# Issuing the gates' and the spilled activations' loads of a PEER layer from ScalarE's queue instead of SyncE's

## The chip, the cores and the metric

The kernel runs on one core of one Trainium2 chip. The metric is the device time of one execution in microseconds (us). A core has five engines that run their own instruction streams in order: TensorE (PE, with its weight loads shown apart as PEld), VectorE (DVE), ScalarE (ACT), GpSimd (POOL) and SyncE (SP). Each stream may also hold instructions that issue a DMA; such an instruction stands in its engine's order like any other, and waits there until the buffer that it fills is free. The profile shows them as SPq, ACTq or POOLq.

## The reference

Two transformer blocks over 512 tokens of 1024 features in float32. The first is differential attention with a hierarchical mixture of experts; the second has a forgetting attention, an RWKV mixer and, at its end, the layer that this case is about: a PEER layer with 16384 single-neuron experts. For each token and head a top-k over product keys picks experts with gates. With the experts numbered in 128 blocks of 128, the layer's output for 384 of the tokens is computed densely:

```
for each block b of 128 experts:
    act[b] = gelu(uT[b]^T x)          # 128 experts x 384 tokens
    W[b]   = act[b] * G[b]            # G: the gates, zero where a token didn't pick the expert
    y     += W[b]^T v[b]              # 384 tokens x 1024
out = layernorm(x * 2^0.25 + y)
```

The last 128 tokens are computed sparsely instead: GpSimd gathers the rows of u and v that each token picked, and VectorE makes the dot products with u and then adds the weighted rows of v.

## The kernel before

Float32 products are made of three matmuls of split operands (`mm3`, L49 to L51: hi x hi, lo x hi, hi x lo). `split` makes the two parts of an operand: the high one on ScalarE (L66), the low one, a subtraction, on VectorE (L67). `load_split` loads a raw tile by `nc.sync.dma_start` (L78) and splits it.

`peer` (L1812) works in two stages. While the gates are being prepared, `spill` computes the activations of the first `NB` = 60 blocks and stores them in DRAM (`hd`); the gates go to DRAM too (`gd`). The last phase is the loop `for z in range(128 + LA)` over all 128 blocks, in the order `order`, which alternates four spilled blocks with four others that are still to be computed (now and then eight of one kind). For each z:

- Every fourth block a tile `G` with the gates of four blocks is loaded (L1917, 768 KB, 2 buffers).
- The block's `act` (3 buffers) is either loaded from `hd` (L1920, 192 KB) or computed by `u_block`: a load of u (512 KB, 3 buffers), its split into `u_hi`, `u_lo`, 24 matmuls of 128x384 into `psu`, and a gelu on ScalarE (L1840).
- VectorE multiplies `act` by the gates in place (L1924); the product is split into `W_hi` (ScalarE) and `W_lo` (VectorE).
- With a lookahead of `LA` = 2, the v of block z - 2 is loaded (512 KB, 3 buffers), split into `v_hi` and `v_lo`, and 18 matmuls of 128x512 add W^T v to the six accumulators `py`.

In between, the steps of the sparse tile are spread over the loop: GpSimd's gathers (L1790), in the first half VectorE's dot products `row<-row,x` (L1797), in the second its sums `x<-row,rg,x` (L1806).

The code is written in the order of the loop; a scheduler puts each engine's instructions in their final order, with the buffers' numbers as its limits. Each engine then runs its list strictly in that order. All loads of the last phase, u, v, G and act, are issued by SyncE.

We call the stretch of eight blocks, four computed and four spilled, a turn. There are 15 turns, some 51 us each; the four computed blocks of a turn are u1 to u4, the four spilled ones s1 to s4. P is the time at which TensorE starts its first `py` matmul after the `psu` matmuls of u4. From P on TensorE has the `py` matmuls of five blocks in a row: u2, u3, u4, s1, s2.

Of the kernel before, what the change touches and what calls it, by code (L numbers as in the profile page):

```python
# [27 lines left out]
class Kern:  # L28
# [1783 lines left out]
    def peer(self, x):  # L1812

        nc, I, tc = self.nc, self.I, self.tc
        NB, ND = 60, NT - 1
        TD = ND * 128
        with ExitStack() as ph:
            dp = ph.enter_context(tc.tile_pool(name="prd", bufs=1, space=DRAM))
            gd = self.t(dp, [2 * ND, 128, 128, 64], F32, "gd")
            hd = self.t(dp, [NB, 128, TD], F32, "hd")  # L1820
# [7 lines left out]
            for kc in range(KC):  # L1828
                p = self.psx()
# [4 lines left out]
            def u_block(b, dst, eng=None):  # L1834

                u = self.load_split(up, I["uT"][b], [128, KC, 128], "u", 3, 3, eng)
                p = self.t(psu, [128, TD], F32, "psu")
                for kc in range(KC):
                    self.mm3(p, [z[:, kc, :] for z in u], [z[:, kc, 0:TD] for z in xT], kc == 0, kc == KC - 1)
                nc.scalar.activation(dst, p, AF.Gelu)  # L1840
# [13 lines left out]
            def run(n):  # L1854
                for step in steps[:n]:
                    step()
                del steps[:n]
# [47 lines left out]
            def blocks(tiles):  # L1905
                for i, W, v in last:
                    for t in tiles:
                        for h in range(2):
                            self.mm3(py[t][h], [y[:, t * 128:(t + 1) * 128] for y in W],
                                     [y[:, h * 512:(h + 1) * 512] for y in v], i == 0, i == 127)  # L1910

            for z in range(128 + LA):
                if z < 128:
                    b = order[z]
                    if b % 4 == 0:
                        G = self.t(wp, [128, 2 * ND, 4, 64], F32, "G", 2)
                        nc.sync.dma_start(G, gd[:, :, b:b + 4, :].rearrange("h p i t -> p h i t"))  # L1917
                    a = self.t(wp, [128, TD], F32, "act", 3)
                    if b < NB:
                        nc.sync.dma_start(a, hd[b])  # L1920
                    else:
                        u_block(b, a)
                    a3 = a.rearrange("p (h t) -> p h t", t=64)
                    nc.vector.tensor_tensor(a3, a3, G[:, :, b % 4, :], OP.mult)  # L1924
                    Ws[b] = self.pair(wp, [128, TD], "W", LA + 3)
                    self.split(Ws[b], a)
                if z >= LA:
                    c = order[z - LA]
                    v = self.load_split(wp, I["v"][c * 128:(c + 1) * 128, :], [128, D], "v", 3, 3)
                    last.append((z - LA, Ws.pop(c), v))  # L1930
                    if z < 128 - 3 + LA:
                        blocks(range(ND))
                        last = []
                    run(len(steps) - max(0, rest - -(-(z - LA + 1) * rest // 122)))
                    if not steps and not ended:
                        ended = True
                        self.layer_norm(wp, x, g, b_, ND, eps)
                        nc.sync.dma_start(self.out[ND * 128:, :], x[:, ND, :])
# [124 lines left out]
```

## Time and profile before

| | |
|---|---|
| median of 3 runs | 2515.73 us (2508.3 to 2515.76) |
| profiled execution, its own time | 2515.3 us |
| its span in the trace | 2513.6 us |
| mean granted clock of TensorE | 0.984 |
| last phase (the loop over 128 blocks) | about 1645 to 2500 us of the span |

The profile is that of one execution, counted from its span's start. An engine's wait is written behind the instruction that followed it, as [us <-what released it]; a table of waits gives for each pair of waiter and releaser the total in us, the number of times and the longest one. In a timeline a row begins with the start and the duration in us; "x2" means two equal instructions back to back, with the time of both.

### The profile page before, as it was taken

How to read it: one execution, taken by the hardware profiler on the slowest of the kernel's cores; microseconds unless marked ns; L12 is line 12 of the kernel's file. 1: busy time of each engine (PE TensorE's matmuls, PEld its weight loads, DVE VectorE, ACT ScalarE, POOL GpSimd, SP SyncE). 2: the span in 40 equal slices, each digit the busy share in tenths (PEclk: the TensorE clock that was granted, in tenths of full speed). 3: DMA queues.
4: the chain of work that ended last, by engine and by line, in shares of the span. 5: the costliest groups of instructions: out<-in, count | busy, mean ns of one | idle time of the engine just before them, and what ended most of it. 6: DMA issues, size and time to landing. Idle time of an engine off the chain costs nothing.

```text
span 2513.6 us, 36164 instructions
## 1 busy us (share of the span) xinstructions
PE 2395.8 (95%) x13502; PEld 1970.5 (78%) x13502; DVE 1924.1 (77%) x3698; ACT 1119.8 (45%) x1651; POOL 553.7 (22%) x458
## 2 busy tenths in 40 slices
PE   8999989999889999999999999989999899999997
PEld 5766666666567777777799989988888789888886
DVE  4577669988867558647699999768787778888786
ACT  3466547777535543224344445533333333333333
POOL 2010112222421100000000000035444444444440
PEclk9999999999999999999999999999999999999999
DMA  7343269999731222225234347899999899999992
GB/s 263 116 166 125 81 228 330 365 366 367 273 105 59 66 72 74 68 60 174 106 115 129 118 151 280 318 360 351 343 336 327 304 331 322 331 338 365 318 334 77
DMA packets 224248, 566.31 MB, mean 225 GB/s; under 512 B 27755, under 2 KB 75924, under 8 KB 223174
## 3 DMA queue, kind: packets, MB, share of 16 engines
q1 hardware_dynamic: 173218, 387.53, 43.7%
q0 software_dynamic: 46048, 166.73, 18.8%
q10 hardware_dynamic: 4804, 9.72, 1.0%
q8 instruction: 107, 1.75, 0.3%
q14 instruction: 71, 0.58, 0.1%
HBM read 511.99 MB, written 51.92 MB: 224 GB/s over the span
## 4 chain that ended last, share of the span: by engine, by line
PE 19%; issue 14%; DVE 12%; POOL 7%; DMA 4%; ACT 1%; POOLq 0%; DVEq 0%; ACTq 0%
POOL row L1790 7%; PE psu L49 3%; PE psu L51 3%; PE psu L50 3%; PE py L50 2%; PE py L51 2%; PE psx L1775 2%; PE py L49 2%; DVE u_lo L67 1%; DMA row<-in_v,ix 1%; DMA act<-hd 1%; DVE x L1806 1%; PE psb L49 1%; PE psb L50 1%; DVE eq L1743 1%
## 5 line engine op out<-in xcount | busy, mean ns | idle before, releaser
L49 PE MATMUL psu<-x4T_hi,u_hi 128*128 128x384 f32 x1024 | 347.1, 339 | 5.6 <-ACT act L1840 4.5
L51 PE MATMUL psu<-x4T_hi,u_lo 128*128 128x384 f32 x1024 | 344.5, 337 | 2.7 <-DVE u_lo L67 2.7
L50 PE MATMUL psu<-x4T_lo,u_hi 128*128 128x384 f32 x1024 | 344.3, 336 | 0.0
L50 PE MATMUL py<-v_lo,W_hi 128*128 128x512 f32 x768 | 303.2, 395 | 17.5 <-DVE v_lo L67 17.5
L49 PE MATMUL py<-v_hi,W_hi 128*128 128x512 f32 x768 | 302.2, 393 | 6.4 <-ACT W_hi L66 5.8
L51 PE MATMUL py<-v_hi,W_lo 128*128 128x512 f32 x768 | 302.3, 394 | 2.2 <-DVE W_lo L67 2.2
L66 ACT ACTIVATE W_hi<-act 128x384 fp32r<-128x384 f32 x128 | 66.4, 525 | 409.1 <-DVE act L1924 408.9
L67 DVE TENSOR_TENSOR ew_lo<-ew_raw,ew_hi 128x2048 fp32r<-128x2048 f32 x93 | 216.8, 2331 | 28.4 <-ACT ew_hi L66 28.3
L1790 POOL DMA_INDIRECT row<-in_v,ix x128 | 181.7, 1420 | 223.4 <-DVE x L1806 189.0
L1790 POOL DMA_INDIRECT row<-in_u,ix x128 | 181.9, 1421 | 222.5 <-DVE dots L1797 204.4
L66 ACT ACTIVATE w_hi<-w_raw 128x1024 fp32r<-128x1024 f32 (+1 forms) x103 | 101.9, 992 | 226.8 <-PE psb L50 147.9
L49 PEld LDWEIGHTS psu<-x4T_hi,u_hi 128*128 128x128 f32 x1024 | 193.3, 189 | 10.1 <-ACT act L1840 4.9
L66 ACT ACTIVATE u_hi<-u_raw 128x1024 fp32r<-128x1024 f32 x128 | 135.0, 1058 | 141.5 <-PE psu L50 124.8
L50 PEld LDWEIGHTS psu<-x4T_lo,u_hi 128*128 128x128 f32 x1024 | 193.4, 189 | 3.7
L51 PEld LDWEIGHTS psu<-x4T_hi,u_lo 128*128 128x128 f32 x1024 | 193.2, 189 | 3.4 <-DVE u_lo L67 3.2
L66 ACT ACTIVATE ew_hi<-ew_raw 128x2048 fp32r<-128x2048 f32 x93 | 178.1, 1916 | 39.8 <-PE psa L51 38.5
L1797 DVE CUSTOM_DVE_ANT_0 row<-row,x 128x1024 f32<-128x1024 f32 x128 | 153.2, 1219 | 45.0 <-DMA row<-in_u,ix 43.5
L50 PEld LDWEIGHTS py<-v_lo,W_hi 128*128 128x128 f32 x768 | 146.0, 190 | 50.4 <-DVE v_lo L67 22.7
L67 DVE TENSOR_TENSOR v_lo<-v_raw,v_hi 128x1024 fp32r<-128x1024 f32 x128 | 156.3, 1221 | 33.3 <-ACT v_hi L66 33.3
L1806 DVE SCALAR_TENSOR_TENSOR x<-row,rg,x 128x1024 f32<-128x1024 f32 x128 | 164.1, 1282 | 18.3 <-DMA row<-in_v,ix 15.2
L49 PEld LDWEIGHTS py<-v_hi,W_hi 128*128 128x128 f32 x768 | 145.7, 190 | 35.6 <-ACT W_hi L66 6.6
L51 PEld LDWEIGHTS py<-v_hi,W_lo 128*128 128x128 f32 x768 | 145.8, 190 | 33.6 <-DVE W_lo L67 3.4
(670 smaller groups left out, 5417.7 us busy)
## 6 DMA issues: line engine op xcount, KB each, us to landing
u_raw<-in_uT SPq DMA_DIRECT2D x128, 512.0 KB
v_raw<-in_v SPq DMA_DIRECT2D x128, 512.0 KB
ew_raw<-in_wgate SPq DMA_DIRECT2D x32, 1024.0 KB
ew_raw<-in_wup SPq DMA_DIRECT2D x32, 1024.0 KB
ew_raw<-in_wdown SPq DMA_DIRECT2D x32, 1024.0 KB
gd<-Gs SPq DMA_DIRECT2D x6, 4096.0 KB
G<-gd SPq DMA_DIRECT2D x32, 768.0 KB
w_raw<-in_w2b SPq DMA_DIRECT2D x39, 512.0 KB
```

The costliest lines, as they stand in the source:

```text
L49: mm(out, L[0], R[0], start=start, stop=False)
L50: mm(out, L[0], R[1], start=False, stop=False)
L51: mm(out, L[1], R[0], start=False, stop=stop)
L66: nc.scalar.activation(hl[0], src, AF.Copy)
L67: (eng or nc.vector).tensor_tensor(hl[1], src, hl[0].bitcast(F32), OP.subtract)
L1743: nc.vector.tensor_tensor(e4, e4, tf[:, s, :, :, None].to_broadcast([128, NT, 16, 16]), OP.mult)
L1775: nc.tensor.matmul(p[:, u, :], A[j], B[i][j], start=i == 0, stop=i == 1)
L1790: keep(nc.gpsimd.indirect_dma_start(r, None, I[name], bass.IndirectOffsetOnAxis(ap=ix[:, h, j:j + 1], axis=0)))
L1797: keep(nc.vector.tensor_tensor_reduce(r, r, x[:, t, :], 1.0, 0.0, OP.mult, OP.add, dots[:, h, j:j + 1]))
L1806: keep(nc.vector.scalar_tensor_tensor(x[:, t, :], r, g[:, h, j:j + 1], x[:, t, :], OP.mult, OP.add))
```

## The change

In the loop of the last phase the loads of G and of the spilled `act` are issued by ScalarE (`nc.scalar.dma_start`) instead of SyncE. These are 32 loads of G and 60 of `act`. The loads of u and v stay on SyncE. No buffer and no arithmetic is changed.

```
--- before.py
+++ after.py
@@ -1914,10 +1914,10 @@
                     b = order[z]
                     if b % 4 == 0:
                         G = self.t(wp, [128, 2 * ND, 4, 64], F32, "G", 2)
-                        nc.sync.dma_start(G, gd[:, :, b:b + 4, :].rearrange("h p i t -> p h i t"))
+                        nc.scalar.dma_start(G, gd[:, :, b:b + 4, :].rearrange("h p i t -> p h i t"))
                     a = self.t(wp, [128, TD], F32, "act", 3)
                     if b < NB:
-                        nc.sync.dma_start(a, hd[b])
+                        nc.scalar.dma_start(a, hd[b])
                     else:
                         u_block(b, a)
                     a3 = a.rearrange("p (h t) -> p h t", t=64)
```

The scheduler's order moves with it. TensorE's and GpSimd's lists have the same instructions as before. In the pieces below, a turn of the second half, act_20277 is the activation of u4, and act_20347, act_20384, act_20421 and act_20458 are those of s1 to s4; v_20430 is the v of s1, v_20467 that of s2 (the numbers differ by one or two between the parts of a tile).

ScalarE's list, from the gelu of u4 on:

```order
 L1840 ACTIVATE act_20277<-psu_20284 128x384
+L1920 DMA act_20347<-hd_11323 128x384
+L1920 DMA act_20384<-hd_11323 128x384
 L66 ACTIVATE W_hi_20311<-act_20277 128x384
-L66 ACTIVATE v_hi_20430<-v_raw_20428 128x1024
+L1917 DMA G_20495<-gd_11322 128x6x256
 L66 ACTIVATE W_hi_20350<-act_20347 128x384
 L66 ACTIVATE W_hi_20387<-act_20384 128x384
+L1920 DMA act_20421<-hd_11323 128x384
+L66 ACTIVATE v_hi_20430<-v_raw_20428 128x1024
+L1920 DMA act_20458<-hd_11323 128x384
+L66 ACTIVATE v_hi_20467<-v_raw_20465 128x1024
```

The loads of s1 and s2 now stand behind the gelu of u4, the load of s3 behind W_hi of s1 and of s2, and the v_hi of s1 and s2 behind the load of s3.

VectorE's list in the same turn, from the multiply of s1 on:

```order
 L1924 TENSOR_TENSOR act_20347<-act_20347,G_20345 128x384
 L1924 TENSOR_TENSOR act_20384<-act_20384,G_20345 128x384
-L67 TENSOR_TENSOR v_lo_20431<-v_raw_20428,v_hi_20430 128x1024
 L67 TENSOR_TENSOR W_lo_20351<-act_20347,W_hi_20350 128x384
 L67 TENSOR_TENSOR W_lo_20388<-act_20384,W_hi_20387 128x384
+L67 TENSOR_TENSOR v_lo_20431<-v_raw_20428,v_hi_20430 128x1024
 L1924 TENSOR_TENSOR act_20421<-act_20421,G_20345 128x384
 L1806 SCALAR_TENSOR_TENSOR x_2268_11033<-row_20452,rg_11399,x_2268_11033 128x1024
 L67 TENSOR_TENSOR W_lo_20425<-act_20421,W_hi_20424 128x384
 L1806 SCALAR_TENSOR_TENSOR x_2268_11033<-row_20455,rg_11399,x_2268_11033 128x1024
+L1924 TENSOR_TENSOR act_20458<-act_20458,G_20345 128x384
 L67 TENSOR_TENSOR v_lo_20468<-v_raw_20465,v_hi_20467 128x1024
```

The v_lo of s2 (v_lo_20468) stands behind the multiply of s3, as before, and now behind the multiply of s4 too.

SyncE's list in the same turn:

```order
 L78 DMA u_raw_20925<-in_uT 128x1024
 L78 DMA v_raw_20535<-in_v 128x1024
-L1920 DMA act_20347<-hd_11323 128x384
-L1920 DMA act_20384<-hd_11323 128x384
 L78 DMA u_raw_20993<-in_uT 128x1024
-L1920 DMA act_20421<-hd_11323 128x384
-L1917 DMA G_20495<-gd_11322 128x6x256
 L78 DMA v_raw_20603<-in_v 128x1024
-L1920 DMA act_20458<-hd_11323 128x384
 L78 DMA v_raw_20674<-in_v 128x1024
-L1917 DMA G_20772<-gd_11322 128x6x256
```

The loads of act and G leave the list, and those of u and v close up.

## Rows read from the trace of the kernel before

**Rows 1.** Windows, the last phase in two halves: columns PE, PEld, DVE, ACT, POOL, PEclk, DMA share, GB/s.
```profile
1650.00:2050.00 400.00, 375.54 (x1789) 329.07 (x1788) 309.80 (x460) 133.27 (x183) 177.40 (x124) 0.98 0.93 336
2050.00:2450.00 400.00, 394.53 (x1902) 347.61 (x1902) 328.21 (x352) 139.91 (x193) 178.94 (x126) 0.99 0.93 333
```

**Rows 2.** Waits of PE from 1640 us on: total, times, longest.
```profile
PE py L50 <- DVE v_lo L67: 17.5, 13, 3.4
PE py L49 <- ACT W_hi L66: 5.8, 1, 5.8
PE psu L49 <- ACT act L1840: 4.5, 1, 4.5
...
PE py L51 <- DVE W_lo L67: 2.2, 1, 2.2
```

**Rows 3.** Timeline of PE, one turn: its P, and v_lo's first use for s2.
```profile
2132.86 0.39 PE L49 MATMUL py<-v_hi,W_hi 128*128 128x512 f32 x1
...
2149.41 0.39 PE L50 MATMUL py<-v_lo,W_hi 128*128 128x512 f32 x1
```

**Rows 4.** Timeline of DVE, the same turn, from the multiply of s3.
```profile
2142.53 0.56 DVE L1924 TENSOR_TENSOR act<-act,G 128x384 f32<-128x384 f32 x1 [2.13 <-DMA act<-hd]
...
2145.87 1.22 DVE L67 TENSOR_TENSOR v_lo<-v_raw,v_hi 128x1024 fp32r<-128x1024 f32 x1
```

**Rows 5.** Tile act: what its engines were idle for (us, times).
```profile
  DMA act<-hd: 50.4, 26
```

**Rows 6.** Timeline of SP, the same turn.
```profile
2131.62 1.06 SPq L1920 DMA_DIRECT2D act<-hd  x2
...
2136.85 0.32 SPq L1920 DMA_DIRECT2D act<-hd  x1
2137.22 0.44 SPq L1917 DMA_DIRECT2D G<-gd  x1
```

**Rows 7.** Waits of SP, 1672 to 2460 us: the largest.
```profile
SPq L78 <- DVE v_lo L67: 376.5, 117, 8.9
```

**Rows 8.** Tile yd, an earlier phase: a DMA that ACT issues, ns min/median/max.
```profile
L952 ACTq DMA_DIRECT2D yd<-yexp x14: 310/310/327, 401.0 to 653.6; - x14
```

**Rows 9.** Timeline of ACT, the same turn: gelu and W_hi of u4.
```profile
2133.85 0.47 ACT L1840 ACTIVATE act<-psu 128x384 f32<-128x384 f32 x1
2135.71 0.53 ACT L66 ACTIVATE W_hi<-act 128x384 fp32r<-128x384 f32 x1 [1.39 <-DVE act L1924]
```

**Rows 10.** Timelines of SP and DVE in the last turn: s1 and s2.
```profile
2389.97 0.90 SPq L1920 DMA_DIRECT2D act<-hd  x2
...
2395.18 1.03 DVE L1924 TENSOR_TENSOR act<-act,G 128x384 f32<-128x384 f32 x2 [0.34 <-DMA act<-hd]
```

**Rows 11.** Timelines of SP and DVE: act issued well behind G.
```profile
1942.31 0.37 SPq L1917 DMA_DIRECT2D G<-gd  x1
1948.95 0.32 SPq L1920 DMA_DIRECT2D act<-hd  x1
...
1954.20 0.56 DVE L1924 TENSOR_TENSOR act<-act,G 128x384 f32<-128x384 f32 x1 [1.13 <-DMA act<-hd]
```

**Rows 12.** Timelines of SP and DVE: act issued 1.6 us behind G (2339.40).
```profile
2341.00 0.32 SPq L1920 DMA_DIRECT2D act<-hd  x1
...
2349.64 0.56 DVE L1924 TENSOR_TENSOR act<-act,G 128x384 f32<-128x384 f32 x1 [5.65 <-DMA act<-hd]
```

**Rows 13.** Timeline of DVE, a turn of the first half: s3's multiply to v_lo.
```profile
1844.82 0.56 DVE L1924 TENSOR_TENSOR act<-act,G 128x384 f32<-128x384 f32 x1 [2.75 <-DMA act<-hd]
...
1849.67 1.22 DVE L67 TENSOR_TENSOR v_lo<-v_raw,v_hi 128x1024 fp32r<-128x1024 f32 x1
```

**Rows 14.** Windows about PE's waits at 1899, 2251 and 2354 us; columns as above.
```profile
1886.00:1906.00 20.00, 17.06 (x69) 13.58 (x68) 14.08 (x24) 6.14 (x9) 6.97 (x6) 0.91 0.82 268
...
2246.00:2256.00 10.00, 8.18 (x30) 6.25 (x29) 8.77 (x10) 3.90 (x5) 4.23 (x4) 0.83 0.86 284
2348.00:2358.00 10.00, 6.94 (x23) 5.08 (x23) 8.37 (x10) 3.89 (x5) 5.04 (x3) 0.83 0.70 235
```

More of the change, by code (lines that the diff above doesn't have):

```diff
@@ L1916, in peer @@
                         G = self.t(wp, [128, 2 * ND, 4, 64], F32, "G", 2)
-                        nc.sync.dma_start(G, gd[:, :, b:b + 4, :].rearrange("h p i t -> p h i t"))
+                        nc.scalar.dma_start(G, gd[:, :, b:b + 4, :].rearrange("h p i t -> p h i t"))
                     a = self.t(wp, [128, TD], F32, "act", 3)
                     if b < NB:
-                        nc.sync.dma_start(a, hd[b])
+                        nc.scalar.dma_start(a, hd[b])
                     else:
```

## Prediction

> **What bounds the kernel now.** I read the windows of the last phase first. TensorE is busy 375.5 of 400 us in its first half and 394.5 of 400 in its second [rows 1], so the phase can't lose more than some 30 us by any better feeding, and whatever makes TensorE wait adds to the time one for one. The DMA engines' share is 0.93 in both halves: a load that is issued late has no idle bandwidth to catch up with. VectorE is the second engine, with 310 and 328 of 400 us.
>
> Next the waits of TensorE [rows 2]. Two stand apart from the turns: 4.5 us for a gelu, at the phase's start, and 5.8 us for a W_hi, once, at 2004 us. The rest, 17.5 us for v_lo in 13 waits and 2.2 us for a W_lo, belongs to the turns: 19.7 us over 15 turns, 1.3 us each. To see what is late there, one turn: TensorE starts the five blocks of py at P = 2132.86 and needs the v_lo of s2 at 2149.41, at P + 16.55 [rows 3]; the time between holds 73 matmuls and nothing else. That v_lo ran at 2145.87, behind the multiply of s3, which VectorE could start only at 2142.53, after 2.13 us of idling for its load [rows 4]. The load is what is late: in all turns the engine that multiplies sat idle 50.4 us for landings of act [rows 5]. So a turn is decided by when the act of s3 lands. In this turn v_lo was done at 2147.09, 2.3 us in time; SyncE had issued s1 and s2 at P - 1.2 (2131.62) and s3 at P + 4.0 (2136.85), just ahead of G [rows 6].
>
> SyncE itself mostly waits for buffers: 376.5 us for v_lo, which frees the raw buffer that the next load of v fills [rows 7]. Those loads are early or late by their own buffers, not by the act and G between them.
>
> **The change, part by part.** *Removed from SyncE:* 92 issues, some 0.3 to 0.5 us each [rows 6]. A load of v or u that waits for its own buffer isn't issued earlier by that, so I cost this gain at nothing in the turns. At the phase's start, where SyncE's list holds a G among the loads of u, the 4.5 us wait [rows 2] could vanish; a G that now goes beside the first u could as well cost what a G costs an act today, 3.4 us (8.6 less 5.25, below). I take 0 of -4.5 to +3.4.
>
> *Added to ScalarE:* 92 issues at 0.31 us [rows 8], 29 us in all. ScalarE is busy 133 and 140 of 400 us [rows 1], so the issues by themselves are covered by its idle time; without that cover they would cost at most the 29 us.
>
> *Moved:* what matters is behind what the loads now wait. In ScalarE's list the loads of s1 and s2 stand behind the gelu of u4, and that of s3 behind the W_hi of s1 and of s2, which themselves wait for the first two loads and two multiplies on VectorE. Before, SyncE needed only a free buffer. So two load latencies now lie one behind the other:
>
> - The gelu of u4 ends at 2133.85 + 0.47, P + 1.46 [rows 9]. s1 and s2 are issued there, 2.7 us later than now.
> - From the issue to the multiply of s1: 5.2 us at the quickest [rows 10], 8.6 us where a G goes just ahead [rows 12]. Here G is issued behind them, so I take 5.7, near the lower end: P + 7.16.
> - Two multiplies 1.03 [rows 10], then W_hi of s2, 0.53 [rows 9] and a handover, together 0.6: P + 8.8. Now s3 is issued, at P + 8.8 instead of P + 4.0.
> - Its landing: 5.25 us where G had been issued 6.6 us ahead [rows 11], 8.6 where it had been 1.6 us ahead [rows 12]. In the new list G goes some 6.5 us ahead, so 5.25: P + 14.05.
> - From the multiply of s3 to the end of v_lo: in the turn shown 2142.53 to 2147.09, 4.56 us, and the multiply of s4, which now stands ahead of v_lo, adds 0.47 (what the second of two multiplies adds to 0.56 where the pair takes 1.03 [rows 4, 10]): 5.03. In the first half, where dot products stand in between and s4's multiply is ahead of v_lo already, 1844.82 to 1850.89, 6.07 us [rows 13].
>
> This gives v_lo at P + 19.1 in the second half and P + 20.1 in the first, against the need at P + 16.55: waits of 2.5 and 3.6 us. Seven turns at 2.5 and eight at 3.6 make 46.3 us. The 19.7 us of today's waits have the same place and are replaced, not added to: +26.6.
>
> *The clock.* After three of today's waits the granted clock falls: 0.91 over 20 us, 0.83 over 10 us and again 0.83 over 10 us [rows 14], 1.7 to 1.8 us lost each time, 5 in all. Such a stretch is one in which TensorE ran at the lower of its two levels (1.2 GHz against 2.4) for a part of the time after a wait. Not every wait does it. If half of the 15 new ones do: 7.5 x 1.7 = 12.8, less 5.1, +7.7.
>
> Sum: 2515.3 + 26.6 + 7.7 = 2549.6, against the profiled execution's own 2515.3, which is the median's 2515.73 but for 0.4. I say 2549. With the quickest landings everywhere (waits of 2.0 and 3.1, 38.8 in all) and no clock loss it is +19, 2534; with one of the two landings in every second turn at 8.6 (some 3 us, 7.5 times) +57, 2572.
>
> The Trainium skill speaks against this sum: "DMA: Bandwidth & Descriptors", section "Issuing engines are not separate DMA queues", says that DMAs started from different engines run on the same 16 DMA engines and that starting them elsewhere only saves the sequencer's issue time. By that alone the change would be worth next to nothing, and the time stay at 2515. But the same page, in the section "Anatomy of one DMA — SWDGE (gpsimd) path", says that a semaphore wait happens on the issuing sequencer before dispatch; by that a load inherits the waits of the list that it stands in, which is what the rows of SyncE show too [rows 7].
>
> **The rivals.**
>
> *The loads no longer queue behind u and v (faster).* On SyncE an act stands behind loads of 512 KB and their waits for buffers; from a queue of its own it could land sooner than 5.25 us after the issue, and u and v close up. If s3 landed before P + 11.5 (16.55 less 5.03) in every turn, the 19.7 us and the start's 4.5 would go and 5 of clock loss with them: 2486. For s3 issued at P + 8.8 this asks a landing within 2.7 us, and the quickest seen is 5.2 [rows 10]; or a first landing so quick that s3 is issued by P + 6.3, which asks 3.2 us there. With the DMA share at 0.93 [rows 1] I give it 0.10.
>
> *It comes to nothing (same).* If the two landings were 0.9 us quicker each than I take, 4.8 and 4.35 us, every turn would wait 1.8 us less, 27 in all, and the 46.3 would be today's 19.7: 2515. Neither was seen so quick [rows 10, 11], but both come close: 0.10. The Trainium skill's rule on issue time would end here too.
>
> *G and act share the DMA engines (slower still).* Today G goes behind s3 in the turn shown [rows 6]; in the new list G always goes ahead of s3, and both compete with v and u from the other queue, which no longer wait behind them. If s3 takes 8.6 us in every turn [rows 12], the waits are 5.9 and 7.0 us: 97 in all, +77 and some 10 of clock, 2602. Half of the turns so: 2575. I give 0.25 to landings like these in at least half of the turns.
>
> **How the numbers follow.** My case, landings near the lower rows, 0.55; the slower one 0.25; same 0.10; faster 0.10. Slower by over 0.3% (7.5 us, about what a measurement can tell from no change) is then 0.80, within it 0.10, faster 0.10. The predicted time is that of my case. The range leaves out the faster rival and the worst of the slower one: from 2520 (the quickest landings, no clock loss and the start's gain are 2530, and 10 us for turns in which a landing is quicker still) to 2580.
>
> **What would show it right or wrong.** In the trace after: the load of s3 issued by ACTq some 9 us after P, behind W_hi of s2; waits of TensorE for v_lo of 2 to 4 us in nearly every turn, some 46 us in the table; idle time of act's engine for act<-hd well above 50.4 us; the last phase longer, everything before 1620 us as it was; and SyncE's waits for v_lo and u_lo grown, since their buffers come free as late as TensorE is. It is wrong if s3 lands before P + 11.5 in most turns, if the v_lo of s1 (which now stands behind the W_lo of s2, at about P + 11.5 with a need at P + 12.5) is the one that is waited for, or if u is late at the start.

## The result, and the profile after

The changed kernel takes 2545.77 us (median of 4 runs, 2544.77 to 2554.16) against 2513.52 before (median of 4, 2508.3 to 2515.76): a ratio of 1.013, 95% interval 1.011 to 1.0151, some 32 us slower. The forecast was 2549.

The profiled execution is the slowest of the four, 2554.16 us, with a span of 2552.5, 38.9 more than that of before. Not all of this is the change's: the last store of gates, which ends the stage ahead of the last phase, is issued at 1626.5 us here and at 1618.5 before, and up to there every engine runs the same instructions in the same order in both. From that store to the end it is 925.9 us against 895.1, +30.8, and this stretch ("the phase" below) is what the traces are compared by. It divides, with a turn counted from the end of VectorE's multiply of u4, into the time up to the first turn (66.5 us against 62.9), the time from the first turn to the last (789.1 against 763.5, +25.6) and the rest (70.3 against 68.7).

The windows of the changed kernel, columns as in [rows 1]; the second stretch is 440 us long:

```profile
1650.00:2050.00 400.00, 366.75 (x1709) 320.08 (x1708) 297.60 (x439) 129.25 (x175) 163.94 (x120) 0.96 0.90 325
2050.00:2490.00 440.00, 419.50 (x2014) 369.35 (x2013) 347.36 (x378) 150.20 (x204) 193.75 (x132) 0.98 0.89 321
```

TensorE idles 33 and 20 us, its granted clock is lower in the first half, and the DMA engines are less busy than before (0.90 and 0.89, where both halves had 0.93): in the mean they have no more to do, it is single loads that are waited for.

TensorE's waits from 1640 us on, as in [rows 2], and the rows of the tile act as in [rows 5], with how ScalarE issued its loads and how long they took to land:

```profile
PE py L50 <- DVE v_lo L67: 35.8, 14, 6.4
PE psu L49 <- ACT hs L1840: 8.7, 3, 4.3
PE py L49 <- ACT W_hi L66: 4.4, 1, 4.4
PE py L51 <- DVE W_lo L67: 3.2, 2, 2.9
```

```profile
L1920 ACTq DMA_DIRECT2D act<-hd x60: 326/327/1189, 1688.8 to 2485.3; - x60
...
  DMA act<-hd: 73.2, 28
...
DMA to landing us min/median/max: 2.4/5.7/10.9
```

The waits for v_lo have doubled, from 17.5 us to 35.8, and VectorE stood idle 73.2 us for landings of act instead of 50.4. At the start TensorE now waits 8.7 us for gelus of the last spilled blocks (hs) where it waited 4.5 for an act. The single wait of 4.4 us for a W_hi was 5.8 before. It belongs to one turn, at 2004 us before and 2020 us here, in which VectorE's list waits for gathered rows of the sparse tile (5.28 us before, 5.20 here) ahead of the multiply of u4.

One turn of the second half, the last `psu` matmul of u4, the list of ScalarE and then that of VectorE, P = 2263.47:

```profile
2263.29 0.34 PE L51 MATMUL psu<-x4T_hi,u_lo 128*128 128x384 f32 x1
```

```profile
2263.49 1.06 ACT L66 ACTIVATE u_hi<-u_raw 128x1024 fp32r<-128x1024 f32 x1 [1.98 <-PE psu L50]
2263.67 0.81 ACTq L1920 DMA_DIRECT2D act<-hd  x2
2264.45 0.47 ACT L1840 ACTIVATE act<-psu 128x384 f32<-128x384 f32 x1
...
2266.93 0.38 ACTq L1917 DMA_DIRECT2D G<-gd  x1
2269.39 1.00 ACT L66 ACTIVATE W_hi<-act 128x384 fp32r<-128x384 f32 x2 [1.95 <-DVE act L1924]
2269.92 0.33 ACTq L1920 DMA_DIRECT2D act<-hd  x1
```

```profile
2266.33 0.55 DVE L1924 TENSOR_TENSOR act<-act,G 128x384 f32<-128x384 f32 x1
...
2279.46 0.56 DVE L1924 TENSOR_TENSOR act<-act,G 128x384 f32<-128x384 f32 x1 [6.84 <-DMA act<-hd]
...
2283.27 1.21 DVE L67 TENSOR_TENSOR v_lo<-v_raw,v_hi 128x1024 fp32r<-128x1024 f32 x1
```

and TensorE at its end:

```profile
2284.53 0.79 PE L50 MATMUL py<-v_lo,W_hi 128*128 128x512 f32 x1 [4.36 <-DVE v_lo L67]
```

s3 is issued at 2269.92, 3.0 us behind G, and lands only for the multiply at 2279.46; v_lo is done at 2284.48, P + 21.0, and TensorE waits 4.4 us. Since P itself moves with TensorE's waits, turns are compared from the end of u4's multiply (2266.88 here). Worked out over all 15 turns, s3 is issued 3.2 us after it (median; before 1.2) and multiplied 10.7 us after it (before 8.1). From its own issue to its multiply it takes 6.55 us in the median, as in the kernel before (6.47): as the change has it, s3 is issued later, and doesn't take longer from there.

### The profile page after: what moved, and what is told of

Its sections match the earlier page's. It is cut to its first block, busy times and chain, and to the rows that moved or that the text cites. A ratio compares the mean times of both kernels' runs of the same rounds, so it can differ in the third digit from the quotient of the medians.

```text
span 2552.5 us, 36142 instructions
## 1 busy us (share of the span) xinstructions
PE 2414.6 (95%) x13502; PEld 1985.2 (78%) x13502; DVE 1925.2 (75%) x3698; ACT 1124.4 (44%) x1651; POOL 552.4 (22%) x458
## 3 DMA queue, kind: packets, MB, share of 16 engines
q0 software_dynamic: 46048, 166.73, 18.5%
## 4 chain that ended last, share of the span: by engine, by line
issue 19%; PE 16%; DVE 10%; POOL 8%; DMA 3%; ACT 1%; POOLq 0%; DVEq 0%; ACTq 0%
POOL row L1790 8%; PE psu L49 2%; PE psu L51 2%; PE psu L50 2%; DMA row<-in_v,ix 2%; PE psx L1775 2%; DVE u_lo L67 1%; PE py L50 1%; PE py L51 1%; PE py L49 1%; PE psb L49 1%; DMA act<-hd 1%; PE psb L50 1%; PE psb L51 1%; DVE eq L1743 1%
## 5 line engine op out<-in xcount | busy, mean ns | idle before, releaser
L50 PE MATMUL py<-v_lo,W_hi 128*128 128x512 f32 x768 | 307.4, 400 | 35.8 <-DVE v_lo L67 35.8
L1790 POOL DMA_INDIRECT row<-in_v,ix x128 | 187.6, 1465 | 234.1 <-DVE x L1806 196.3
L1790 POOL DMA_INDIRECT row<-in_u,ix x128 | 175.3, 1370 | 241.5 <-DVE dots L1797 222.0
L66 ACT ACTIVATE v_hi<-v_raw 128x1024 fp32r<-128x1024 f32 x128 | 134.2, 1053 | 146.4 <-DMA v_raw<-in_v 85.5
L1806 DVE SCALAR_TENSOR_TENSOR x<-row,rg,x 128x1024 f32<-128x1024 f32 x128 | 164.1, 1282 | 15.5 <-DMA row<-in_v,ix 13.9
L51 PEld LDWEIGHTS py<-v_hi,W_lo 128*128 128x128 f32 x768 | 148.3, 193 | 35.1 <-DVE W_lo L67 4.1
```

The lines of the kernel that those rows point to most:

```text
L50: mm(out, L[0], R[1], start=False, stop=False)
L51: mm(out, L[1], R[0], start=False, stop=stop)
L66: nc.scalar.activation(hl[0], src, AF.Copy)
L1790: keep(nc.gpsimd.indirect_dma_start(r, None, I[name], bass.IndirectOffsetOnAxis(ap=ix[:, h, j:j + 1], axis=0)))
L1806: keep(nc.vector.scalar_tensor_tensor(x[:, t, :], r, g[:, h, j:j + 1], x[:, t, :], OP.mult, OP.add))
```

## Experiments

The measured medians beside each other, with the 15 turns of each profile: where G goes, when s3 is multiplied (median after the end of u4's multiply), VectorE's idle time for act, and the phase.

| | median us | ratio to before, 95% | G goes | s3's multiply | idle for act | phase |
|---|---|---|---|---|---|---|
| before | 2513.52 | | behind s3 | 8.1 | 50.4 | 895.1 |
| the change | 2545.77 | 1.011 to 1.0151 | ahead | 10.7 | 73.2 | 925.9 |
| e1, G only | 2555.0 | 1.0108 to 1.0192 | ahead | 9.4 | 73.7 | 929.6 |
| e2, act only | 2538.9 | 1.0062 to 1.0128 | ahead | 9.3 | 74.7 | 920.2 |
| e3, change with 4 + 2 buffers | 2495.28 | 0.9897 to 0.9945 | | | 15.1 | 875.0 |
| e4, before with 4 + 2 buffers | 2490.45 | 0.9874 to 0.9934 | | | 21.6 | 868.9 |
| e5, change, VectorE's order held | 2549.25 | 1.0121 to 1.0167 | ahead | 10.1 | 69.0 | 925.7 |
| e6, change, loads' order of before | 2525.11 | 1.003 to 1.0059 | behind s3 | 7.4 | 37.8 | 908.3 |
| e7, G only, VectorE's order held | 2538.7 | 1.0053 to 1.0108 | ahead | 9.9 | 60.4 | 918.9 |
| e8, SyncE, G first | 2511.87 | 0.9979 to 1.0007 | ahead | 10.3 | 54.5 | 887.9 |
| e9, change, short chain | 2533.77 | 1.0069 to 1.0104 | ahead | 10.5 | 67.8 | 913.3 |
| e10, before, short chain | 2513.15 | 0.9991 to 1.0015 | behind s3 | 8.0 | 50.8 | 892.1 |
| e11, change, start's order | 2540.13 | 1.0085 to 1.0124 | ahead | 10.0 | 66.2 | 920.9 |
| e12, e6 with G ahead | 2550.61 | 1.0121 to 1.0168 | ahead | 11.0 | 77.1 | 928.2 |

("The change" was compared with its own four runs of before, the others with runs of before on their chips, medians 2512.51 to 2514.17.)

**e1 and e2: one half of the change each.** Only the first, or only the second of its two lines:

```
e1: -nc.sync.dma_start(G, gd[:, :, b:b + 4, :]...)
    +nc.scalar.dma_start(G, gd[:, :, b:b + 4, :]...)
e2: -nc.sync.dma_start(a, hd[b])
    +nc.scalar.dma_start(a, hd[b])
```

> Only the 32 loads of G move to ScalarE's queue; the act loads stay with SyncE. Theory A (the act loads are late because of what they wait behind in ScalarE's list): s3 is issued by SyncE about 1.2 us after the multiply of u4 as before, so most of the loss is gone: 2514 to 2524 us, waits of TensorE in the turns near the 19.7 us of before. Rival B (G, now issued at the W_hi of u4 ahead of s3, takes the DMA engines from s3): s3 lands 8 us or more after its issue, waits of 40 us in the turns, 2535 to 2545 us.

> Only the 60 act loads move to ScalarE's queue; G stays with SyncE. Theory A: s3 is issued 2 to 4 us after the multiply of u4 instead of 1.2, and most of the loss of 31 us stays: 2535 to 2545. Rival B: without G ahead of it s3 lands in 5 us, and the loss is gone: 2514 to 2524.

Both came out slow, 2555.0 and 2538.9, so the halves don't add up and neither theory fits alone. The traces have it: in both, s3 is issued where it was before (1.2 us after u4's multiply), and in both G now goes ahead of it. On ScalarE G is issued at the W_hi of u4; on SyncE, with the act loads gone from the list, it moves up to the same place. s3 then takes 7.7 and 7.8 us from its issue to its multiply instead of 6.5. So e2, which lies in theory A's range, lies there for another reason.

**e3 and e4: the loads well ahead.** The tile of act split in two, on the changed kernel and on that of before:

```
-a = self.t(wp, [128, TD], F32, "act", 3)
+a = self.t(wp, [128, TD], F32, "acl" if b < NB else "act", 4 if b < NB else 2)
```

> The changed kernel with 4 buffers for the loaded act and 2 for the computed ones, in place of 3 for both: a load no longer waits for the buffer of a computed block and is issued most of a turn ahead, still by ScalarE. Theory A: the waits for v_lo in the turns (36 us) go nearly all, and the time falls below that of before: 2488 to 2502. Rival C (two hardware queues: u and v lose bandwidth to act and G on the other queue, whatever the order): waits for v or u remain, 2515 or more.

> The kernel before with the same buffers (4 for loaded act, 2 for computed), all loads on SyncE. Theory A: as e3 within 5 us, 2488 to 2502, since the queue doesn't matter once the loads are early. Rival C: 15 us or more faster than e3.

As theory A had it: with early loads the queue hardly matters (the two intervals overlap), and both beat the kernel before, e4 by 24 us. The pair doesn't tell A from B, though: s3 is now issued some 20 us before the multiply of u4 ends (medians 20.9 and 17.4), and the G that stood ahead of it goes behind it, so that it is out of G's way too. The waits of e4 in the last phase:

```profile
PE py L49 <- ACT W_hi L66: 7.2, 1, 7.2
PE psu L49 <- ACT act L1840: 3.7, 1, 3.7
PE psu L51 <- DVE u_lo L67: 1.9, 1, 1.9
PE psu L49 <- ACT hs L1840: 1.3, 2, 0.7
PE py L50 <- DVE v_lo L67: 1.0, 2, 0.8
```

Of the 17.5 us for v_lo 1.0 is left. That the act landed late is what the turns waited for in the kernel before as well.

**e5 and e7: VectorE's order.** The change moved VectorE's list too (the multiply of s4 stands ahead of the v_lo of s2 in all 15 turns, before in 5 of them; in e1 and e2 the v_lo of s1 also stands behind the multiply of s3, in 13). Here the orders that most turns of before have are held in all of them, in the changed kernel (e5) and in e1 (e7), by edges that fix an issue order on one engine and wait for nothing. `mi`, `vi`, `wi`, `li`, `gi` hold by z the multiply, the two parts of v and of W, and the loads of act and G; s is the z of s1 (in this and the cuts that follow, the conditions around the lines are left out):

```
+def behind(ins, first):
+    tc.add_manual_dep(ins, first.name, ...)
...
+behind(mi[s + 2], vi[s + 2][1])
+behind(mi[s + 3], vi[s + 3][1])
```

> The changed kernel, with two orders on VectorE held as they were before: the multiply of s3 behind the v_lo of s1 and the multiply of s4 behind the v_lo of s2. ScalarE's and SyncE's lists stay those of the changed kernel. Theory A (the load of s3 is late on ScalarE's list): only the 0.47 us of the multiply of s4 comes back in each turn, 2538 to 2545 us. Rival D (what the scheduler puts ahead of v_lo on VectorE is the loss): 2514 to 2522.

> G alone on ScalarE's queue (as e1, where 2555 was measured), with VectorE's order held as in e5. Rival B (G, issued ahead of s3, takes the DMA engines from it): s3 lands some 1.3 us later than before, about 20 us over 15 turns, 2530 to 2540. Rival D (VectorE's order): all of it goes, 2514 to 2522. If neither matters, it stays at 2550 to 2558.

e5 gave nothing back (2549.25): VectorE's order isn't the loss of the change. e7 did, 16 us of e1's 41; the rest stays, as rival B had it, with G on ScalarE ahead of s3, which is multiplied 8.7 us after its issue.

**e6 and e12: where s3 and G stand on ScalarE's list.** In both the load of s3 is held ahead of the W_hi of s1, so that it waits for nothing but its buffer, as before, and VectorE's order is that of e5. In e6 G is held behind s3 too:

```
+behind(wi[s][0], li[s + 2])
...
+behind(gi[z], li[z - 2])
```

> All loads of G and act on ScalarE's queue as in the change, but in the places they had before: the load of s3 held ahead of the W_hi of s1, G held behind the load of s3, and the two orders on VectorE of e5. Theory A: the queue by itself costs nothing, 2512 to 2522 us. Rival C (a second hardware queue or ScalarE's issuing is what costs): 2535 or more.

> As e6 (act and G on ScalarE's list, the load of s3 held ahead of the W_hi of s1, VectorE's order held), but G stays ahead of s3 as in the change. Theory A (what counts is where s3 is issued): as e6, 2518 to 2530. Rival B (G ahead of s3 on the second queue delays its landing): as e7, 2533 to 2542.

This pair, one edge apart, decides between the two places of G. Both issue s3 at 1.2 us after u4's multiply, 2 us earlier than the change. One turn of e12, ScalarE and then VectorE:

```profile
2206.70 0.38 ACTq L1923 DMA_DIRECT2D G<-gd  x1
2207.84 0.33 ACTq L1927 DMA_DIRECT2D act<-hd  x1
2209.30 0.99 ACT L66 ACTIVATE W_hi<-act 128x384 fp32r<-128x384 f32 x2 [2.08 <-DVE act L1931]
```

```profile
2219.52 0.56 DVE L1931 TENSOR_TENSOR act<-act,G 128x384 f32<-128x384 f32 x1 [7.01 <-DMA act<-hd]
```

and one of e6:

```profile
2307.07 0.33 ACTq L1927 DMA_DIRECT2D act<-hd  x1
2307.71 0.53 ACT L66 ACTIVATE W_hi<-act 128x384 fp32r<-128x384 f32 x1 [1.26 <-DVE act L1931]
...
2309.61 0.61 ACTq L1923 DMA_DIRECT2D G<-gd  x1
```

```profile
2313.06 0.56 DVE L1931 TENSOR_TENSOR act<-act,G 128x384 f32<-128x384 f32 x1 [1.54 <-DMA act<-hd]
```

With G 1.1 us ahead, s3 takes 11.7 us to its multiply; with G 2.5 us behind, 6.0. The medians over the turns are 9.8 and 6.1. e12 is as slow as e5, where s3 stood behind both W_hi: an s3 that is issued 2 us earlier behind G is multiplied no earlier. So theory A doesn't explain the loss; taking G out of the way of s3 gives 25 us back between the medians (20 between the two profiles, of which e6's is the slowest of its ten runs). Both missed their forecasts by a little: e6 lies 3 us above A's 2522, e12 9 us above B's 2542.

The other traces agree. In the nine profiles with three-buffer act in which G goes ahead, s3 is multiplied 9.2 to 11.0 us (medians) after the issue of G, whether s3 is issued 1.1 us behind G (e1, e2, e7, e8, e12) or 2.6 to 3.6 (the change, e5, e9, e11). What no run has is an s3 that is late on ScalarE's list with G behind it, so what a late issue costs by itself isn't known.

e6 is still 11 us slower than the kernel before. In its profile some 6 us of that are the time up to the first turn, of which more at e11, and 8 us lie in the turns. VectorE's list of e6 has one more sum of the sparse tile between the multiply of s3 and v_lo in two turns, so that it isn't quite that of before.

**e8: G first on SyncE.** The kernel before with the load of s3 held behind G, and e5's order on VectorE:

```
+behind(li[z - 2], gi[z])
```

> All loads on SyncE as before, but G held ahead of the load of s3, and VectorE's order held as in e5. Rival B: the same loss as in e7 without any second queue, 2530 to 2540 us. If it takes the second queue for G to hurt: 2514 to 2522.

s3 landed as late as in e7 (multiplied 8.6 us after its issue), and yet the time is that of before, 2511.87. So a late s3 isn't enough. One turn of e8, SyncE and then VectorE:

```profile
2230.31 0.37 SPq L1923 DMA_DIRECT2D G<-gd  x1
2231.46 0.32 SPq L1927 DMA_DIRECT2D act<-hd  x1
```

```profile
2234.78 1.28 DVE L1807 SCALAR_TENSOR_TENSOR x<-row,rg,x 128x1024 f32<-128x1024 f32 x1
2241.57 0.56 DVE L1931 TENSOR_TENSOR act<-act,G 128x384 f32<-128x384 f32 x1 [5.50 <-DMA act<-hd]
2242.04 1.28 DVE L1807 SCALAR_TENSOR_TENSOR x<-row,rg,x 128x1024 f32<-128x1024 f32 x1
2243.24 0.55 DVE L67 TENSOR_TENSOR W_lo<-act,W_hi 128x384 fp32r<-128x384 f32 x1
2243.71 1.22 DVE L67 TENSOR_TENSOR v_lo<-v_raw,v_hi 128x1024 fp32r<-128x1024 f32 x1
```

In the scheduler's order for e8 a sum stands ahead of the multiply, in time in which VectorE would idle. Over the 15 turns, 13 sums or dots are left between the multiply of s3 and the v_lo; in e7 there are 30. From the multiply to the end of v_lo it is 3.4 us in this turn and 3.3 in the median; in e7 the median is 4.55. That is 1.2 us a turn, 18 in all. TensorE's waits for v_lo, in e8 and then in e7:

```profile
PE py L50 <- DVE v_lo L67: 13.8, 8, 2.8
...
PE py L50 <- DVE v_lo L67: 29.7, 11, 5.0
```

The phases of e7 and e8 differ by 31 us, 7 of them up to the first turn and 24 in the turns. So VectorE's order can be the greater part of it, but that is argued: the reading that the forecast of e8 has for such a time, that G hurts from a second queue only, is refuted for the landing of s3 and not for the time.

**e9 and e10: a short chain by force.** The sums and dots that the loop emits at s3 (`ri`) are held behind the v_lo of s2, beside e5's order, in the changed kernel and in that of before:

```
+for i in ri.get(s + 2, []):
+    behind(i, vi[s + 3][1])
```

> The changed kernel with VectorE's sums and dot products of the sparse tile held behind the v_lo of s2, so that this v_lo follows the multiply of s3 at once (about 1.7 us from the multiply's start to its end, in place of 5 to 6); the loads stay late on ScalarE's list. Theory E (what TensorE pays is the landing of s3 plus what stands on VectorE between its multiply and v_lo): 3.3 us or more less in each turn, 2508 to 2522. If v_lo is late for another reason (its own load of v, the queue): 2535 or more.

> The kernel before with the same hold on VectorE (2.2 us from the multiply of s3 to the end of v_lo), all loads on SyncE. Theory E: most of the 19.7 us that the turns wait goes, and the clock's part with it, 2488 to 2500. If the waits come from elsewhere: 2508 to 2518.

Both missed: e9 got 12 us of the 24 or more, e10 nothing, though from s3's multiply to the end of v_lo it is only 1.7 us in e9 and 3.3 in e10 (medians; 5.0 in the change, 4.55 before). The waits of e10 for py:

```profile
PE py L50 <- DVE v_lo L67: 11.4, 8, 5.7
PE py L49 <- ACT W_hi L66: 7.3, 3, 5.8
PE py L49 <- ACT v_hi L66: 3.1, 4, 1.2
```

v_lo's went from 17.5 to 11.4, but others came (v_hi 3.1 where it had been 0.6, two more for W_hi), and s1's multiply stands 1.0 us later after P in the median. The sums that were moved behind v_lo delay what follows on VectorE. That time comes back only where they go into VectorE's idle time, as in e8, is a reading that fits e7 to e10, but no run changed it alone.

**e11: the start.** The change with the v_hi of the first six blocks of the loop held behind the last gelu of a spilled block:

```
+if z < 128 and z - LA < 6:
+    behind(vi[z][0], last_hs)
```

> The changed kernel with one order on ScalarE held at the phase's start: the v_hi of the first blocks behind the gelus of the last spilled blocks, as they stood before. Theory F (the start's loss is TensorE waiting for gelus behind a v_hi whose load is late): the 8.7 us of waits for hs go, 4 to 8 us in all, 2538 to 2543, and the stretch from the last store of gates to the first turn falls from 66.6 us to 59 to 63. If the loss is G's bandwidth: unchanged, 2544 to 2550.

The median, 2540.13, is in the forecast, but not by what was forecast: the time to the first turn is 68.3 us, no shorter than the change's 66.5, and the interval overlaps that of the change. Inconclusive as a gain; theory F is not borne out. In the profiles with three-buffer act that time is 61.6 to 62.9 us where G is on SyncE (before, e2, e8, e10) and 66.5 to 69.5 where it is on ScalarE (the change, e1, e5 to e7, e9, e11, e12).

The traces show where these 4 to 8 us may come from. The second G in the kernel before, and then both of the change with the first v_hi behind them:

```profile
1653.74 0.43 SPq L1917 DMA_DIRECT2D G<-gd  x1
```

```profile
1641.09 0.38 ACTq L1917 DMA_DIRECT2D G<-gd  x1
...
1643.28 0.37 ACTq L1917 DMA_DIRECT2D G<-gd  x1
...
1657.46 1.06 ACT L66 ACTIVATE v_hi<-v_raw 128x1024 fp32r<-128x1024 f32 x1 [7.59 <-DMA v_raw<-in_v]
```

On SyncE the second G stands behind loads of u and v and is issued 35.3 us after the last store of gates; on ScalarE it is issued 16.7 us after it, 2.2 us behind the first. So it is in all profiles: 35.1 to 36.4 us in the five with G on SyncE, 15.5 to 17.0 in the nine with G on ScalarE, and the third load of v, at 35.6 to 37.9 us there, is issued at 43.1 to 44.1 here. In e11 the v_hi is out of the way of the gelus, but ScalarE waits 9.23 us for a store of hs instead. This is again a G that goes ahead of more urgent transfers, as e11's other branch had it for the start; no run held the second G back, so it is argued and not shown.

## Why the prediction was right, and where it wasn't

The time, the direction and the place were right: 2545.77 against 2549, lost in the turns, as waits for the v_lo of s2 behind the multiply of s3. Term by term:

- **The turns' waits.** Forecast 46.3 in place of 19.7, +26.6. Measured 35.8 and 3.2 in place of 17.5 and 2.2: +19.3. Right in kind, the size over a third too large.
- **The clock.** Forecast +7.7. From the first turn to the last it is +25.6; less the waits some 6 us are left, with PEclk 0.96 and 0.98 where it was 0.98 and 0.99 [rows 1]. Right in size; the 6 is a remainder, not a measurement of the clock.
- **The start.** Forecast 0, measured +3.6, just beyond the end that I had given (+3.4), which stood for a G that goes beside the first u. The second G does go 18.5 us earlier than before (16.7 us after the last store of gates for 35.3).
- **SyncE.** Its waits for v_lo grew from 376.5 [rows 7] to 463.6 us, as forecast: having the list to themselves, u and v still wait for their buffers.
- **When v_lo is done.** Forecast P + 19.1 and P + 20.1; the median of the 15 turns is P + 19.1. This agreement is luck, made of two errors. The step "s3 issued at P + 8.8" failed: the median is P + 6.6. The loads of s1 and s2 didn't wait for the gelu that stands ahead of them (2263.67 against 2264.45 in the turn above), P + 0.2 in place of P + 1.46, the multiply of s1 came 5.1 us later in place of 5.7, and s3 followed early. The landing that I took for s3, 5.25 us, failed the other way: issue to multiply is 6.55 in the median. Nor was the 5.2 us of [rows 10] the quickest landing of s1 before: that turn is the last but one, and in the last it is 4.78 us (issue at 2441.21, multiply at 2445.99), which the rival of no change had as unseen.
- **The mechanism.** "Two load latencies one behind the other" was the step on which the sum stood. The trace has both in a row, and s3 is issued late by it, but e12 shows that this isn't what costs the time: without it s3 is multiplied no earlier. What holds s3 back is the third rival's mechanism, G ahead of s3 on shared DMA engines, which I had priced at a landing of 8.6 us in at least half of the turns, and given 0.25. Its price isn't what was measured either: s3's own landing in the change stays at 6.55 us, because s3 follows G late. The row for it was there, a turn of the kernel before in which G went first [rows 12]; I took the one with G 6.6 us ahead [rows 11], because by the false step s3 would go that late. In fact s3 follows G by 3.2 us in the median.
- **The turn shown.** The turn at 2132.86 [rows 3, 4] was an easy one: in most turns of before, s1 was issued at P + 0.8 and s3 at P + 6.3 (medians), not at P - 1.2 and P + 4.0. A median over the turns would have shown that s3 could be issued little later than it already was.

The Trainium skill's rule in "DMA: Bandwidth & Descriptors", section "Issuing engines are not separate DMA queues", that all of these loads run on the same 16 DMA engines and interleave, agrees with e12 against e6: the same 192 KB take 9.8 or 6.1 us by what goes ahead of them. Its other half, that only issue time is saved, says nothing of the loss here, which comes of the order in which loads go.

What is shown: the act loads' landing is what the turns wait for (e3, e4), and on ScalarE's list G ahead of s3 is what made it late (e6 against e12). What is argued: why the same order on SyncE costs nothing (e8), by VectorE's filled idle time, and that the 4 to 8 us at the start come of the second G. Left open: what a late issue of s3 costs without a G ahead of it, and the 8 us that e6 loses in the turns.

## What to carry to other kernels

Moving loads to another queue changes which goes first, and a big load that slips ahead of a small urgent one can cost more than the move gains (25 us here, e12 against e6): before moving, ask which load is waited for, and see that nothing large is issued just ahead of it. Where a wait is for a landing, more buffers did here what another queue didn't: e4, with 4 buffers for the loaded tile and 2 for the computed one, all loads on SyncE, is the fastest here at 2490.45 us. And read such a wait as a distribution over the turns, not from one turn.

## What the runs showed of the hardware

A DMA issue on ScalarE's list doesn't wait until the ACTIVATE that stands ahead of it has run, but it does wait for what that ACTIVATE waits for. In the turn shown the two loads were issued from 2263.67 us on, 0.04 us after the last `psu` matmul of u4 had ended (2263.29 + 0.34), while a u_hi ran, and the gelu ahead of them in the list, which needs that matmul, started at 2264.45. In all 15 turns it is 0.04 us behind that matmul and 0.78 to 0.90 us ahead of the gelu, and the load of s3 is issued at most 0.06 us behind the start of the W_hi of s2 (2269.92 in the turn shown, in which the second of the two W_hi starts at 2269.86). So "strictly in that order" doesn't hold between an issue and the execution of the instruction ahead of it.

A load of 192 KB takes from 2.4 to 12.2 us to land in one phase of one kernel (e12), with medians of 5.6 to 6.7 in the runs with three-buffer act whose traces tell it (7.5 and 8.6 in e4 and e3, where the loads go far ahead); the number that matters is that of the one load that is waited for.
